# Five gate tiles instead of four held back for the end of attention, and a fourth raw weight buffer

## The chip, the cores and the metric

The kernel runs on one core of one Trainium2 chip. The metric is device time in microseconds for one launch, the median over several runs. The program names are those of the engines: TensorE (PE, with its weight loads as PEld), VectorE (DVE), ScalarE (ACT), GpSimd (POOL), and SyncE (SP), which issues nearly all DMAs from one queue (SPq).

## The reference

Two layers work on 528 tokens (16 learned ones and 512 of the sequence) of width 1024. Each layer normalises, makes one large input projection, mixes tokens in two ways, and adds the gated sum of both back:

```python
h = rmsnorm(h_res, norm_gain[l])
proj = h @ w_in[l]
u_pool, z_pool, c_q, c_kv, k_rope, z_mla, g_pool, g_mla = jnp.split(proj, IN_SPLIT_POINTS, axis=-1)
y_pool = (pool_mix(u_pool, pool_w_group[l], pool_scale[l]) * jax.nn.silu(z_pool)) @ pool_w_up[l]
o_mla = mla(c_q, c_kv, k_rope, pos, q_a_norm_gain[l], kv_a_norm_gain[l], w_q_b[l], w_kv_b[l],
            q_norm_gain[l], k_norm_gain[l])
y_mla = (o_mla * jax.nn.silu(z_mla)) @ mla_w_up[l]
merged = jax.nn.sigmoid(g_pool) * y_pool + jax.nn.sigmoid(g_mla) * y_mla
h_res = h_res + merged @ w_out[l]
```

`mla` is causal attention with 8 heads (96 query and key dimensions, 64 value dimensions). `pool_mix` takes means over windows of 2, 4, 8 and 16 tokens.

## The kernel before, in words

**Tiles.** Features lie on the 128 partitions, tokens along the free dimension. A projection to 128 output features is a "tile", named after its part of the layer: `u`, `zp`, `cq`, `pu`, `zm`, `gp0` to `gp7` (the pooling gate), `gm0` to `gm7` (the attention gate), `mu` (attention's up projection), `o` (the output). A gate tile has 8 blocks of 128 input features. Layer 0 takes the tokens in two halves of 264, each with a PSUM bank of its own; layer 1 drops the learned tokens and takes 512 at once.

**Every product is three matmuls.** Full precision comes from splitting weights and activations into a high and a low float32r part. `mm3` (lines 211 to 213) issues high x high, high x low and low x high. So a gate tile has 48 matmuls in layer 0 and 24 in layer 1.

**Weights.** `wload` brings 512 columns, half of a gate tile, from HBM into a `raw` buffer (three of them, line 140; the load is issued by SyncE on line 136), ScalarE makes the high part `whi` (line 206) and VectorE the low part `wlo` (line 207). There are three buffers each of `whi` and `wlo`. A raw buffer is free when line 207 has read it. Loads run four chunks ahead of the matmuls in the program. SyncE's queue is in order: a load that waits for its buffer holds back all that stands behind it.

**Filler.** `stream` is a generator of all projections in a fixed order; each `step` emits a few of its matmuls and moves a planner's clock `clk` by 1/2.4 ns per column. The attention code calls it in its gaps. `fill(ns, limit)` lets the clock run up by `ns` per call, but not past the end of the tile named `limit`; `fill_now(ns)` has no limit. `gap` (line 1159) calls `fill` with `FILL[layer]` and `RESERVE[layer]`. One head has four gaps, two in `head` and two in `go`, so a layer has 32. Whatever the gaps leave is run after the last head.

**One head.** `head` issues the scores of four query blocks in three PSUM banks `S`: blocks 1 and 3 (in part) in the first, block 2 in the second, the rest of block 3 and block 0 in the third. VectorE adds the mask and takes the row maximum (line 843), ScalarE takes the exponential (line 850), VectorE transposes in blocks of 32 (line 856). SyncE writes the result to HBM (`pdr`, line 916) and reads it back rearranged (`attE`, line 924), with the row sums by `rdr` (written on line 927, read on line 934). `parts` splits what came back (ScalarE line 972, VectorE line 973), and `pv` multiplies with the values (lines 994 and 997) into the one bank `o`. ScalarE and VectorE move its two halves together (lines 1002 and 1003). After each second head, one more matmul for the learned tokens follows (line 1009), which VectorE adds and gates (lines 1012 and 1013).

**The end of a layer's attention** (in `go`): the round trip of the last head through HBM is covered by `fill_now(TAIL[layer])`, then `parts`, 2600 ns more, and the last `pv`. What is left of `gm` follows, and then `mu`, which needs all heads.

**Banks.** The projections share four PSUM banks `mm`, used in turn. Those of `gp` are emptied by VectorE line 665, those of `gm` by VectorE line 1058.

**Order.** Within each engine the instructions run in the printed order. A scheduler with its own timeline sets it from the program's order and its dependencies, so a change of the gap lengths moves instructions on all engines.

The constants and `rawt` as they stand before are in the listing that follows.

Of the kernel before, what the change touches and what calls it, by code (L numbers as in the profile page):

```python
# [9 lines left out]
F32 = mybir.dt.float32  # L10
# [8 lines left out]
P = 128  # L19
# [31 lines left out]
G_H, G_CKV, G_CQ, G_QN, G_QR, G_KN, G_KR, G_PS = 0, 8, 10, 16, 17, 18, 19, 20  # L51
N_GAIN = 24

FILL = (2583.0, 2493.0)
RESERVE = ("gm3", "gm3")
LAG = 2000.0
TAIL = (9000.0, 9000.0)
SPL = 240
BACK = 7800.0
LATE = 13000.0  # L60
# [21 lines left out]
def trunk(ctx, tc, xT, xrow, mrow, pos, win, wkr, wqb, wkb, wvb, wgr, wpu, wmu, wout, gains, const, yT):  # L82
# [5 lines left out]
    wp = ctx.enter_context(tc.tile_pool(name="wp", bufs=2))  # L88
# [7 lines left out]
    def nm(s):  # L96
        uid[0] += 1
        return f"{s}_{uid[0]}"
# [38 lines left out]
        return raw  # L137

    def rawt():
        return wp.tile([P, 512], F32, tag="raw", name=nm("raw"), bufs=3)  # L140

    early.append(slot("rinv"))
    act.dma_start(early[0][:, 0:512], win[0, MT_CKV, :, 0:512])
    first = sp.dma_start(gn, gains)
    sp.dma_start(xb[:, 0, :T], xT[:, 0, :])
    early.append(fetch(win[0, MT_CKV + 1, :, 0:512], 512, rawt(), sp))
    sp.dma_start(xb[:, 1, :T], xT[:, 1, :])
    xt = [xb[:, k] for k in range(8)]
# [16 lines left out]
    def other_loads(made):  # L165
        for k in range(2, 8):
            behind(sp.dma_start(xb[:, k, :T], xT[:, k, :]), made)
            if k in (3, 4):
                raw = rawt()
                behind(sp.dma_start(raw, win[0, MT_CKV + k - 3, :, 512:1024]), made)  # L170
                early.append(raw)
        behind(sp.dma_start(cst, const), made)
        behind(sp.dma_start(posb[:, :T], pos.partition_broadcast(P)), made)
        dve.tensor_copy(maskw[:, 512 - P:], cst[:, C_MASK:C_MASK + P])
# [18 lines left out]
    def wload(src, n, spare, home=None):  # L193
        if home is not None:
            raw = home
            behind(sp.dma_start(raw, src), marks[-4])
        else:
            raw = early.pop(0) if early else fetch(src, n, rawt(), sp)
        loads[0] += 1
        marks.append(newest[0])  # L200
        if loads[0] <= 2 or spare:
            t = wide()
            hi, lo = t[:, 0:512], t[:, 512:1024]
        else:
            hi, lo = (wp.tile([P, 512], F32R, tag=t, name=nm(t), bufs=3) for t in ("whi", "wlo"))
        act.activation(hi[:, :n], raw[:, :n], AF.Copy)  # L206
        dve.tensor_sub(lo[:, :n], raw[:, :n], hi[:, :n].bitcast(F32))  # L207
        return hi, lo
# [87 lines left out]
    def fill(ns, limit):  # L296
        if due[0] is None:
            due[0] = clk[0]
        due[0] += ns
        while clk[0] < due[0] and limit not in done and step():  # L300
            pass

    def fill_now(ns):
        end = clk[0] + ns
        while clk[0] < end and step():
            pass
# [47 lines left out]
    class Layer:  # L354
# [804 lines left out]
        def gap(self):  # L1159
            fill(FILL[self.l], (self.l, RESERVE[self.l]))  # L1160

        def go(self, nxt):
# [54 lines left out]
            if not self.last:  # L1217
                self.meta_queries()
            fill_now(TAIL[self.l])
            late = self.parts(now)  # L1220
# [87 lines left out]
```

## Time and profile before

| | us |
|---|---|
| median of 3 runs | 753.75 |
| lowest and highest of them | 753.75, 754.27 |
| the profiled execution's own time | 755.48 |
| its span, first to last instruction | 753.7 |
| layer 0, TensorE, first score matmul of head 0 to the last of head 7's third bank | 175.63 to about 279.8 |
| layer 0, last P.V begins | 303.98 |
| layer 1, first masks to those of head 7 | 560.3 to 655.6 |

In the profile, busy times of matmuls overlap, since the next one starts while one drains; what a matmul costs is read from the distance of two starts. A row of the timeline gives start, duration, engine, line, operation and tile. "Idle before" in square brackets names what ended the idle time.

### The profile page before, as it was taken

To read this page: it belongs to the slowest core of one execution; us is meant where nothing else is said; L and a number is where in the kernel's file an instruction comes from. 1 tells how busy PE (TensorE), PEld (TensorE's weight loads), DVE (VectorE), ACT (ScalarE), POOL (GpSimd) and SP (SyncE) were. 2 spreads that over 40 slices of the span, in tenths; PEclk is the share of its full clock that TensorE was granted. 3 is DMA by queue.
4 is the path that set the end of the run, shared out by engine and by line. 5 is a ranking of instruction groups with operands and counts; after the bars stand their busy time and mean duration, and the time that the engine had idled before them with its cause. 6 is when DMAs were issued, how large, how long until landed. Compare 5 with 4: busy or idle time off the path is not lost.

```text
span 753.7 us, 14317 instructions
## 1 busy us (share of the span) xinstructions
PE 748.1 (99%) x5010; PEld 681.9 (90%) x5010; DVE 562.3 (75%) x1214; ACT 395.2 (52%) x864; POOL 241.8 (32%) x294
## 2 busy tenths in 40 slices
PE   9999999999999999999999999999999999999998
PEld 9999899999999999999997898887788888887887
DVE  5588777658999987694367478678589999966942
ACT  6755656554656555543254456455445665554321
POOL 2126404704552520161130264038043526102400
PEclk9999999999999999999999999999999999999999
DMA  8633223434766576425643332233356666763462
GB/s 280 179 103 118 70 81 91 112 96 142 206 163 177 170 202 176 129 91 165 183 135 91 108 113 73 82 91 107 105 151 216 181 175 189 203 167 98 129 223 87
DMA packets 72798, 106.55 MB, mean 141 GB/s; under 512 B 14051, under 2 KB 34915, under 8 KB 72726
## 3 DMA queue, kind: packets, MB, share of 16 engines
q1 hardware_dynamic: 72582, 105.38, 47.8%
q8 instruction: 39, 0.64, 0.4%
q14 instruction: 33, 0.27, 0.1%
q10 hardware_dynamic: 144, 0.26, 0.1%
HBM read 89.76 MB, written 15.85 MB: 140 GB/s over the span
## 4 chain that ended last, share of the span: by engine, by line
PE 94%; DMA 4%; SPq 1%; DVE 1%; ACT 0%; issue 0%; ACTq 0%; DVEq 0%
PE mm L211 28%; PE mm L213 28%; PE mm L212 28%; PE S L211 2%; PE S L213 2%; PE S L212 2%; DMA raw<-wmu 1%; PE o L994 1%; DMA rdr<-rs 1%; PE o L997 1%; PE S L891 1%; PE S L538 1%; PE S L504 0%; DMA raw<-win 0%; DMA cq<-rdr 0%; DMA xb<-xT 0%
## 5 line engine op out<-in xcount | busy, mean ns | idle before, releaser
L213 PE MATMUL mm<-hh,wlo 128*128 128x264 f32 (+2 forms) x1072 | 337.0, 316 | 0.0
L212 PE MATMUL mm<-hl,whi 128*128 128x264 f32 (+2 forms) x1072 | 336.4, 315 | 0.0
L211 PE MATMUL mm<-hh,whi 128*128 128x264 f32 (+2 forms) x1072 | 336.3, 315 | 0.0
L207 DVE TENSOR_TENSOR wlo<-raw,whi 128x512 fp32r<-128x512 f32 (+2 forms) x239 | 179.6, 754 | 87.5 <-ACT whi L206 83.9
L206 ACT ACTIVATE whi<-raw 128x512 fp32r<-128x512 f32 (+2 forms) x239 | 143.0, 600 | 167.3 <-PE mm L212 133.2
L211 PEld LDWEIGHTS mm<-hh,whi 128*128 128x128 f32 x1072 | 201.4, 188 | 14.1 <-DVE vt L704 0.8
L212 PEld LDWEIGHTS mm<-hl,whi 128*128 128x128 f32 x1072 | 201.6, 188 | 13.0
L213 PEld LDWEIGHTS mm<-hh,wlo 128*128 128x128 f32 x1072 | 200.9, 188 | 12.3
L652 POOL TENSOR_TENSOR racc<-racc,tmp 128x264 f32<-128x264 f32 (+1 forms) x15 | 14.9, 993 | 117.7 <-ACT tmp L651 117.7
L1069 POOL TENSOR_TENSOR tmp<-tmp,xb 128x264 f32<-128x264 f32 (+1 forms) x24 | 27.7, 1166 | 41.8 <-DVE tmp L1067 39.7
L821 POOL CAST qhl<-q 32x528 fp32r<-32x528 f32 (+1 forms) x32 | 27.6, 876 | 40.5 <-PE S L891 39.1
L843 DVE CUSTOM_DVE_ANT_0 S<-S,maskw,nqs 128x240 f32<-128x240 f32 (+4 forms) x80 | 37.9, 493 | 1.5 <-PE S L213 1.3
L211 PE MATMUL mm<-cq,whi 128*128 128x264 f32 (+1 forms) x108 | 34.7, 321 | 0.0
L212 PE MATMUL mm<-th,whi 128*128 128x264 f32 (+1 forms) x108 | 34.6, 321 | 0.0
L213 PE MATMUL mm<-u,wlo 128*128 128x264 f32 (+1 forms) x108 | 34.5, 320 | 0.0
L212 PE MATMUL mm<-cq,whi 128*128 128x264 f32 (+1 forms) x108 | 34.5, 321 | 0.0
L213 PE MATMUL mm<-cq,wlo 128*128 128x264 f32 (+1 forms) x108 | 34.5, 321 | 0.0
L211 PE MATMUL mm<-u,whi 128*128 128x264 f32 (+1 forms) x108 | 34.5, 319 | 0.0
L938 POOL TENSOR_TENSOR u<-u,cq 128x512 f32<-128x512 f32 x8 | 12.9, 1616 | 64.6 <-DMA cq<-rdr 41.2
L853 POOL COPY pm<-cq 128x16 f32<-128x16 f32 x32 | 17.9, 559 | 44.4 <-ACT cq L850 42.3
L850 ACT ACTIVATE cq<-S,bia 128x400 f32<-128x400 f32 (+2 forms) x48 | 24.4, 512 | 13.9 <-DVE bia L904 12.8
L973 DVE TENSOR_TENSOR attE<-attE,th 128x640 fp32r<-128x640 f32 x32 | 25.6, 828 | 6.1 <-ACT th L972 6.1
(305 smaller groups left out, 1401.2 us busy)
## 6 DMA issues: line engine op xcount, KB each, us to landing
raw<-win SPq DMA_DIRECT2D x143, 256.0 KB, 3.5
pdr<-attD SPq DMA_DIRECT2D x16, 640.0 KB, 3.6
attE<-pdr SPq DMA_DIRECT2D x64, 160.0 KB, 3.6
raw<-wout SPq DMA_DIRECT2D x32, 256.0 KB, 3.0
raw<-wpu SPq DMA_DIRECT2D x16, 256.0 KB, 2.7
raw<-wmu SPq DMA_DIRECT2D x16, 256.0 KB, 2.7
raw<-wqb SPq DMA_DIRECT2D x12, 256.0 KB, 2.6
xb<-xT SPq DMA_DIRECT2D x8, 264.0 KB, 5.6
```

What stands on the lines that cost most here:

```text
L206: act.activation(hi[:, :n], raw[:, :n], AF.Copy)
L207: dve.tensor_sub(lo[:, :n], raw[:, :n], hi[:, :n].bitcast(F32))
L211: first = pe.matmul(out, wh, xh, start=start, stop=False)
L212: pe.matmul(out, wh, xl, start=False, stop=False)
L213: newest[0] = pe.matmul(out, wl, xh, start=False, stop=stop)
L652: self.acc_last = gp.tensor_add(self.acc[:, a:b], self.acc[:, a:b], t[:, :b - a])
L821: gp.tensor_copy(d[r0:r0 + 32, x0:T], f[gq:gq + 32, x0:T])
L843: return dve.tensor_tensor_reduce(out=sv, in0=sv, in1=mask, scale=nqs[:, i, h:h + 1], scalar=3e38, op0=ALU.add, op1=ALU.min, accum_out=bia ...
L850: act.activation(pv, sv, AF.Exp, scale=-1.0, bias=bia[:, i:i + 1], accum_out=rs[:, c:c + 1])
L853: gp.tensor_copy(pm[:, i, 16 * odd:16 * odd + 16], pt[i][:, 0:NM])
L973: dve.tensor_sub(got[:, a:b], f[:, a:b], hi[:, a:b].bitcast(F32))
L1069: gp.tensor_add(t[:, :b - a], t[:, :b - a], self.am[m][:, a:b])
```

## The change

```diff
-FILL = (2583.0, 2493.0)
-RESERVE = ("gm3", "gm3")
+FILL = (2217.0, 2145.0)
+RESERVE = ("gm2", "gm2")
 LAG = 2000.0
-TAIL = (9000.0, 9000.0)
+TAIL = (14300.0, 14000.0)
...
     def rawt():
-        return wp.tile([P, 512], F32, tag="raw", name=nm("raw"), bufs=3)
+        return wp.tile([P, 512], F32, tag="raw", name=nm("raw"), bufs=4)
```

Each of the 32 gaps of a layer is shortened by 366 (layer 0) and 348 (layer 1) ns of the planner's clock. The gaps may run the stream to the end of `gm2` instead of `gm3`, so that `gm3` to `gm7` are kept for the end instead of `gm4` to `gm7`. The stretch before the last head's `parts` grows by 5300 and 5000 ns; a gate tile is 5280 ns in layer 0 and 5120 in layer 1 on that clock. And raw weight chunks get a fourth buffer. No operation is added to or taken from TensorE; the printed orders have 4871 rows for it in both.

What the orders show at three places. In a row stand line, operation, what is written <- what is read, and the shape. The first is TensorE in layer 0, head 1: the scores of its third bank (`S_2817` now) and the filler around them, the two token halves of a `zm` tile (`mm_2760`, `mm_2761`). Now:

```order
L213 MATMUL mm_2760<-hh_16_156,wlo_2757 128x264
L211 MATMUL S_2817<-kh_2474,qhl_109 128x288
L212 MATMUL S_2817<-kl_2475,qhl_109 128x288
L213 MATMUL S_2817<-kh_2474,qhl_110 128x288
L891 MATMUL S_2817<-kh_2474,qhl_109 128x144
L891 MATMUL S_2817<-kl_2475,qhl_109 128x144
L891 MATMUL S_2817<-kh_2474,qhl_110 128x144
L891 MATMUL S_2817<-kh_2474,qhl_109 16x16
L891 MATMUL S_2817<-kl_2475,qhl_109 16x16
L891 MATMUL S_2817<-kh_2474,qhl_110 16x16
L211 MATMUL mm_2760<-hh_18_158,whi_2756 128x264
```

Before, these scores stood 15 filler matmuls later, after the end of `mm_2761`. So it is in most heads of layer 0: scores come after less filler.

The second place is where head 6's scores begin in layer 0. On TensorE, now (`mm_3766` and `mm_3767` are the two token halves of one gate tile, `mm_3774` is the learned tokens' matmul of heads 2 and 3, the `S` rows are the first pass of head 6's scores):

```order
L213 MATMUL mm_3766<-hh_18_158,wlo_3763 128x264
L1009 MATMUL mm_3774<-racc_3551,vb_1257 128x512
L211 MATMUL S_3789<-kh_3616,qhl_107 128x272
L211 MATMUL S_3798<-kh_3616,qhl_107 128x400
L211 MATMUL S_3877<-kh_3616,qhl_107 128x288
L211 MATMUL mm_3767<-hh_4_144,whi_3721 128x264
```

With four banks in turn, `mm_3774` takes the bank of `mm_3526`, and `mm_3767` that of `mm_3640`. VectorE's rows that follow the emptying of `mm_3526`, now:

```order
L667 SCALAR_TENSOR_TENSOR xb<-tmp_3630,xb 128x264
L1012 TENSOR_TENSOR tmp_3483<-mm_3774,tmp_3483 128x512
L665 TENSOR_TENSOR tmp_3739<-mm_3640,rinv_585 128x264
L910 RECIPROCAL rs_3560<-rs_3560 128x4
L665 TENSOR_TENSOR tmp_3756<-mm_3641,rinv_585 128x264
L1013 TENSOR_TENSOR tmp_3483<-tmp_3483,u_461_2706 128x512
```

Before, the learned tokens' matmul of these heads (`mm_3884`) stood amid the filler of a tile half, the next tile half opened the bank of `mm_3698`, and VectorE emptied that among the masks of head 5:

```order
L665 TENSOR_TENSOR tmp_3760<-mm_3697,rinv_585 128x264
L843 ISA S_3772,bia_3657<-S_3772,maskw,nqs_2282 128x288
L843 ISA bia_3657 128x1
L665 TENSOR_TENSOR tmp_3825<-mm_3698,rinv_585 128x264
L1003 TENSOR_TENSOR tmp_3570<-o_3800,tmp_3570 64x512
```

What moved: the emptying of `mm_3640` now stands behind the row that reads `mm_3774`, and TensorE comes to `mm_3767` after less filler.

The third place is SyncE's queue at the end of attention in layer 1: row sums of the last head (`rdr`), the learned tokens (`racc`), the last chunk of `gm7` (`win`), the first chunks of `mu` (`wmu`). Before:

```order
L927 DMA rdr_143<-rs_8559 128x4
L136 DMA raw_8853<-win 128x512
L136 DMA raw_8872<-wmu 128x512
L934 DMA cq_1558_8707<-rdr_143 64x512
L136 DMA raw_8901<-wmu 128x512
L955 DMA racc_8817<-mdr 32x4x128 x3
```

Now:

```order
L927 DMA rdr_143<-rs_8474 128x4
L955 DMA racc_8732<-mdr 32x4x128 x2
L934 DMA cq_1540_8621<-rdr_143 64x512
L955 DMA racc_8732<-mdr 32x4x128
L136 DMA raw_8853<-win 128x512
L136 DMA raw_8880<-wmu 128x512
```

The last chunk of `gm7` and the first of `mu` moved from ahead of the read of `rdr`, which waits for its write to land, to behind it.

## The prediction

> **What bounds the kernel now.** I read the page first, then who waited for whom on TensorE, then busy time by stage, then single instructions at the places where TensorE came closest to a wait. The page:
>
> ```profile
> span 753.7 us, 14317 instructions
> PE 748.1 (99%) x5010; PEld 681.9 (90%) x5010; DVE 562.3 (75%) x1214; ACT 395.2 (52%) x864; POOL 241.8 (32%) x294
> ```
>
> TensorE is never free for long, and the matmuls are the same before and after the change. So only pauses between them can be won or lost. The waits of TensorE (waiter, what it waited for, us in total, times, longest), and the timeline of TensorE around the two that lie in the program (start, us, instruction, idle before it):
>
> ```profile
> PE mm L211 <- DVE cq L1058: 1.1, 1, 1.1
> PE S L994 <- ACT th L972: 0.2, 1, 0.2
> ...
> 303.50 0.28 PE L213 MATMUL mm<-hh,wlo 128*128 128x264 f32 x1
> 303.98 0.51 PE L994 MATMUL S<-th,vt 128*128 128x512 f32 x1 [0.19 <-ACT th L972]
> ...
> 686.16 0.40 PE L213 MATMUL mm<-q,th 128*128 128x512 f32 x1
> 687.70 0.47 PE L211 MATMUL mm<-q,whi 128*128 128x512 f32 x1 [1.14 <-DVE cq L1058]
> ```
>
> Starts tell the price of a matmul, since each overlaps the next. In a stretch without waits, 25 steps of 264 columns and 9 steps of 512 (first and last row of each):
>
> ```profile
> 297.03 0.28 PE L211 MATMUL mm<-hh,whi 128*128 128x264 f32 x1
> ...
> 300.07 0.28 PE L212 MATMUL mm<-hl,whi 128*128 128x264 f32 x1
> ...
> 661.71 0.39 PE L212 MATMUL mm<-hl,whi 128*128 128x512 f32 x1
> ...
> 663.79 0.39 PE L212 MATMUL mm<-hl,whi 128*128 128x512 f32 x1
> ```
>
> 3.04 / 25 = 0.1216 us and 2.08 / 9 = 0.231 us. The step 303.50 to 303.98 is 0.48 us, so 0.36 is lost there; 686.16 to 687.70 is 1.54, so 1.31 is lost. About 1.67 us is all that better cover at the two ends of attention can bring.
>
> The second engine matters because of its share inside attention. Busy time by stage, columns as in the header row:
>
> ```profile
> core 0: us, PE busy (x) PEld busy (x) DVE busy (x) ACT busy (x) POOL busy (x), PEclk, DMA share, GB/s
> 175.63:258.36 82.73, 82.73 (x673) 82.07 (x672) 77.46 (x203) 48.96 (x122) 36.41 (x53) 1.00 0.58 166
> 180.60:257.58 76.98, 76.98 (x627) 76.36 (x626) 74.24 (x197) 46.70 (x118) 36.31 (x52) 1.00 0.60 170
> 180.60:291.06 110.46, 110.46 (x895) 109.32 (x894) 105.52 (x289) 68.20 (x176) 42.68 (x65) 1.00 0.62 176
> 175.63:291.48 115.85, 115.85 (x939) 114.71 (x938) 108.44 (x293) 70.31 (x180) 42.79 (x66) 1.00 0.61 174
> 560.30:655.60 95.30, 95.30 (x475) 80.38 (x474) 92.96 (x224) 60.37 (x145) 41.06 (x62) 1.00 0.64 186
> ```
>
> VectorE is busy 105.52 of 110.46 us in the heads of layer 0 and 92.96 of 95.30 in those of layer 1. TensorE has no pause there only because VectorE is just fast enough. How just, two places of layer 0 show, where a matmul opens a PSUM bank that VectorE has emptied a moment before (VectorE row and TensorE row of each):
>
> ```profile
> 257.16 0.42 DVE L665 TENSOR_TENSOR tmp<-mm,rinv 128x264 f32<-128x264 f32 x1
> 258.39 0.28 PE L211 MATMUL mm<-hh,whi 128*128 128x264 f32 x1
> ...
> 290.65 0.41 DVE L1058 TENSOR_TENSOR cq<-mm,rinv 128x264 f32<-128x264 f32 x1
> 291.48 0.28 PE L211 MATMUL mm<-hh,whi 128*128 128x264 f32 x1
> ```
>
> The bank is empty at 257.58 and used at 258.39 (0.81 us to spare); at 291.06 and 291.48 (0.42). That the row pairs share a bank is inferred from the rotation of four banks in the order of first use.
>
> **The change part by part.**
>
> *Less filler between the heads.* FILL falls by 366 and 348 per gap, and each layer has 32 gaps. The printed orders tell what that moves. In layer 0, from head 0's first score block to the second place above, TensorE has 733 filler matmuls before and 685 now: 48 fewer, one gate tile, 48 x 0.1216 = 5.8 us. To the first place (in the changed order the second token half of a gate tile, opened as head 6's scores begin) it is 529 before and 457 now, 72 fewer or 8.8 us, against which three hoisted score matmuls of 272, 400 and 288 columns cost about 0.4 us. So TensorE reaches these places 8.3 and 5.7 us sooner.
>
> VectorE must have done nearly as much by then. Its groups between the heads of layer 0, and two of layer 1 (busy us, mean ns):
>
> ```profile
> L207 DVE TENSOR_TENSOR wlo<-raw,whi 128x512 fp32r<-128x512 f32 x29 | 20.9, 722 | 0.1
> L843 DVE CUSTOM_DVE_ANT_0 S<-S,maskw,nqs 128x272 f32<-128x272 f32 (+4 forms) x40 | 19.3, 491 | 0.6 <-PE S L213 0.5
> L667 DVE SCALAR_TENSOR_TENSOR xb<-tmp,xb 128x264 f32<-128x264 f32 x16 | 7.4, 465 | 0.6 <-ACT tmp L666 0.6
> L665 DVE TENSOR_TENSOR tmp<-mm,rinv 128x264 f32<-128x264 f32 x16 | 6.7, 423 | 0.1
> L1003 DVE TENSOR_TENSOR tmp<-o,tmp 64x512 f32<-64x512 f32 x7 | 4.8, 684 | 0.1
> L1058 DVE TENSOR_TENSOR cq<-mm,rinv 128x264 f32<-128x264 f32 x8 | 3.4, 419 | 0.1
> ...
> L207 DVE TENSOR_TENSOR wlo<-raw,whi 128x512 fp32r<-128x512 f32 x26 | 18.3, 704 | 0.7 <-ACT whi L206 0.7
> L973 DVE TENSOR_TENSOR attE<-attE,th 128x640 fp32r<-128x640 f32 x12 | 9.6, 834 | 0.0
> ```
>
> At the second place VectorE has 287 instructions ahead before and 285 now: three L207 (2.2 us) and two L1058 (0.8) fewer, one each of L1003, L310 and L1013 more (about 0.7 each): 0.9 less. At the first, two L207, three L665 and two L667 fewer (1.4 + 1.3 + 0.9 = 3.6), and an L1003, an L1012, two masks (L843), two transposes and small ones more, about 3.1: 0.5 less. So the spare time becomes 0.81 - 8.3 + 0.5 = -7.0 us at the first place and 0.42 - 5.7 + 0.9 = -4.4 at the second. These are not added: a pause at the first lets VectorE catch up for the second, so the larger decides. The late bank is emptied behind one more wait: VectorE's L1012 stands ahead of that L665, and needs the L1009 matmul of TensorE; behind it queue the other gate evacuations and the next weight split.
>
> What softens it is VectorE's idle time, 76.98 - 74.24 = 2.7 us up to the first place; if a late VectorE never waits, 7.0 shrinks to 4.3. Bounds for layer 0: 4.3 and 7.0. I take 5.5, between them, since part of that idle time is the wait for ScalarE's exponentials, which come no sooner.
>
> In layer 1, up to head 7's last scores the order has 13 filler matmuls fewer (13 x 0.231 = 3.0 us) and one L1009 more (0.2), and VectorE loses one L207 and two L973 (0.7 + 1.7 = 2.4). The two move almost together: 0, from -0.4 to +1.
>
> *TAIL and RESERVE.* The tile that leaves the heads is run before the last head's P.V. In layer 0 it covers the 0.36 us: -0.36. In layer 1 the loss of 1.31 us is another chain, on the chain of waits (start, us) and in SyncE's queue:
>
> ```profile
> 669.51 4.02 DMA rdr<-rs
> 673.61 0.45 SPq L934
> 674.15 5.58 DMA raw<-wmu
> 679.75 0.64 ACT th L206
> 680.41 0.79 DVE th L207
> 681.22 2.70 DMA raw<-wmu
> ...
> 686.86 0.70 DVE cq L1058
> ...
> 671.30 0.43 SPq L136 DMA_DIRECT2D raw<-win  x1
> ...
> 678.03 0.69 DVE L207 TENSOR_TENSOR wlo<-raw,whi 128x512 fp32r<-128x512 f32 x1 [2.33 <-ACT whi L206]
> ...
> 679.68 0.40 PE L213 MATMUL mm<-hh,wlo 128*128 128x512 f32 x1
> ```
>
> SyncE waits for the small write rdr, and the wmu chunk behind it lands at 679.73. Its split frees a raw buffer, only then is the next chunk asked for (681.22), and VectorE's gate evacuation L1058 stands behind that chunk's split. *The fourth raw buffer* takes away the link at 681.22: a gain of 1.31 at most. But the order also moves the last win chunk and the first wmu chunk behind the wait for rdr. By then VectorE is about 2.4 us ahead of before, so rdr would return near 671.2 instead of 673.6, and the win chunk goes out near 672.2 instead of 671.30; its split has 679.68 - 678.72 = 0.96 us to spare, which that uses up. I take -0.7, from -1.3 to +1. At the start and elsewhere the buffer only lets loads go sooner, where TensorE does not wait: 0.
>
> *Sum.* 5.5 + 0 - 0.36 - 0.7 = +4.4 us. Against the profiled execution (span 753.7, its own time 755.48) that is 758.1 of span; its time lies 1.73 above the median of the runs shown, so I put the difference on the median: 753.75 + 4.4 = **758.2 us**. The likeliest case's own range is 4.3 - 1.7 = +2.6 to 7.0 + 1 + 1 = +9 at the outermost, mostly 756 to 761.
>
> **The rivals.** *A, absorbed:* the row pairs do not share the bank I think, and the weight splits, which are made chunks ahead, lend VectorE the time; then only the gains stay, 753.75 - 1.67 = 752.1. It decides if VectorE takes back all its idle time of 110.46 - 105.52 = 4.9 us, which turns -4.4 at the second place into +0.5. For it: the stretch ends in a part with little VectorE work. Against it: the first place stays late even then. Chance 0.12.
>
> *B, a draw:* the pause is there but small, 1 to 3 us, and the two gains pay for it: 753.75 + 2 - 1.67 = 754.1. Chance 0.08.
>
> *C, late in both layers:* in layer 1, too, the spare times between the heads are used up (VectorE is 97.5% busy there), and the win chunk behind rdr comes late: 7.0 + 1 + 1 - 0.36 = +8.6, 762.4. Chance 0.06.
>
> *D, a slow array after the pause:* if a pause of some 5 us in one piece made TensorE come back at half pace for as long, it would lose another 2.5 us: 760.7. All stages above show a granted clock of 1.00, but none of them has such a pause. Chance 0.05. [...]
>
> *E, the same sign without the fourth buffer's gain:* the split weights have three buffers still, so the chunk comes no sooner, and the 1.31 stays: 753.75 + 5.5 - 0.36 = 758.9. It is counted in the forecast's chance of 0.69.
>
> **How the numbers follow.** About 0.2% (1.5 us) is what a measurement of this kernel can tell from no change: faster means below 752.2, slower above 755.3. A gives faster, B the same, the forecast and C and D slower; a little of each neighbour goes over the edge: faster 0.12, same 0.09, slower 0.79. The range should leave out most of A (0.12) and the top of C: 753.0 to 761.0.
>
> **What would show it.** Right: TensorE has waits inside layer 0's heads, from about head 3 on and above all where head 6's scores begin, released by VectorE (L665, L207, L1058), 4 to 7 us in all; VectorE is 97% busy or more from the first to the last head; the 0.36 us at the last P.V. of layer 0 is gone; and at the mu matmuls of layer 1 the wait for L1058 is shorter. Wrong: no TensorE wait above 0.5 us in layer 0's heads (A), waits of the same size in layer 1's heads (C), a clock below 1.00 (D), or pauses released by DMA rather than VectorE, since then the running sums of VectorE are not what decides.

## The result, and the profile after

The changed kernel is slower: 764.45 us median of four runs (764.12 to 764.82), against 754.01 for the kernel before beside it (753.75 to 755.52), a ratio of 1.0132 with a 95% interval of 1.012 to 1.0143. The forecast was 758.2 with a range up to 761.0: right in sign, too small by 6 us. The profiled execution took 764.82 us. Its page:

```profile
span 763.0 us, 14322 instructions
PE 752.2 (99%) x5010; PEld 684.6 (90%) x5010; DVE 560.9 (74%) x1214; ACT 396.6 (52%) x864; POOL 239.9 (31%) x294
```

TensorE has the same 5010 instructions and is busy 4.1 us longer (752.2 against 748.1): matmuls themselves took longer somewhere, for which the forecast's sum had no term. The waits of TensorE in it (waiter, what it waited for, us in total, times, longest):

```profile
PE mm L211 <- DVE tmp L1012: 2.0, 1, 2.0
PE mm L1009 <- DVE tmp L665: 1.6, 1, 1.6
PE mm L211 <- DVE tmp L665: 1.1, 1, 1.1
...
PE mm L1042 <- ACT whi L206: 0.8, 1, 0.8
PE S L994 <- ACT th L972: 0.5, 1, 0.5
PE mm L213 <- DVE wlo L207: 0.4, 1, 0.4
```

The first three lie in layer 0's heads. TensorE there, and where the pace comes back (start, us, instruction, idle before it):

```profile
222.54 0.28 PE L213 MATMUL mm<-hh,wlo 128*128 128x264 f32 x1
223.90 0.36 PE L211 MATMUL mm<-hh,whi 128*128 128x264 f32 x1 [1.08 <-DVE tmp L665]
...
251.13 0.28 PE L213 MATMUL mm<-hh,wlo 128*128 128x264 f32 x1
253.05 0.50 PE L1009 MATMUL mm<-racc,vb 96*128 96x512 f32 x1 [1.63 <-DVE tmp L665]
253.39 0.60 PE L211 MATMUL S<-kh,qhl 96*128 96x272 f32 x3
255.99 0.59 PE L211 MATMUL mm<-hh,whi 128*128 128x264 f32 x1 [2.00 <-DVE tmp L1012]
...
261.44 0.30 PE L211 MATMUL mm<-hh,whi 128*128 128x264 f32 x1
```

By the distance of starts, less the 0.12 us of a step (0.44 for the three score matmuls of 272, 400 and 288 columns), 1.24, 1.79 and 2.16 us are lost at the three places, 5.19 in all. A fourth pause, 0.93, follows at line 1042 at 293.5. VectorE at the second and third place:

```profile
251.83 0.69 DVE L1003 TENSOR_TENSOR tmp<-o,tmp 64x512 f32<-64x512 f32 x1
252.56 0.43 DVE L665 TENSOR_TENSOR tmp<-mm,rinv 128x264 f32<-128x264 f32 x1
252.91 0.70 DVE L310 TENSOR_TENSOR kl<-tmp,kh 128x528 fp32r<-128x528 f32 x1
253.52 0.70 DVE L856 STREAM_TRANSPOSE attD<-cq 128x512 f32<-128x512 f32 x1
...
254.53 0.81 DVE L667 SCALAR_TENSOR_TENSOR xb<-tmp,xb 128x264 f32<-128x264 f32 x1
255.26 0.68 DVE L1012 TENSOR_TENSOR tmp<-mm,tmp 128x512 f32<-128x512 f32 x1
255.86 0.42 DVE L665 TENSOR_TENSOR tmp<-mm,rinv 128x264 f32<-128x264 f32 x1
```

Line 665 empties a bank at 252.99, and line 1009 starts at 253.05. Its own bank is emptied by line 1012, which stands behind a split, a transpose and a gate row and ends at 255.94; the next tile half starts at 255.99, before the L665 below has ended. So it did not wait for that L665, and what fits its start is the bank of the learned tokens' matmul.

The matmuls that took longer lie where the granted clock is low. Busy time by stretch (columns as in the header):

```profile
core 0: us, PE busy (x) PEld busy (x) DVE busy (x) ACT busy (x) POOL busy (x), PEclk, DMA share, GB/s
250.00:254.60 4.60, 2.36 (x16) 1.81 (x14) 4.54 (x13) 2.47 (x8) 3.18 (x6) 1.00 0.39 124
254.60:261.40 6.80, 5.41 (x24) 5.41 (x25) 5.39 (x13) 2.61 (x6) 1.22 (x2) 0.50 0.67 208
261.40:270.00 8.60, 8.60 (x73) 8.55 (x72) 6.68 (x16) 4.73 (x10) 2.53 (x3) 1.00 0.46 138
```

For 6.8 us the granted clock is 0.50. From 255.99 to 261.44 TensorE makes 24 steps in 5.45 us instead of 24 x 0.1216 = 2.92: 2.5 us lost. At the two ends of attention:

```profile
305.23 0.28 PE L212 MATMUL mm<-hl,whi 128*128 128x264 f32 x1
305.36 0.40 PE L994 MATMUL S<-th,vt 128*128 128x512 f32 x1
...
679.06 0.39 PE L212 MATMUL mm<-hl,whi 128*128 128x512 f32 x1
679.96 0.50 PE L994 MATMUL S<-th,vt 128*128 128x512 f32 x1 [0.50 <-ACT th L972]
...
692.45 0.40 PE L212 MATMUL mm<-kn,whi 128*128 128x512 f32 x1
693.28 0.50 PE L213 MATMUL mm<-q,wlo 128*128 128x512 f32 x1 [0.43 <-DVE wlo L207]
```

Layer 0's last P.V starts without loss (-0.36, as forecast). In layer 1 the old pause of 1.31 is gone, but 0.66 and 0.60 stand in its place. These account for 8.2 of the 9.3 us by which the two profiled spans differ: pauses of layer 0 5.19 + 0.93, clock 2.5, last P.V -0.36, layer 1 -0.05. Of the other 1.1, half was there before the first head (head 0's scores at 176.2 against 175.63); the rest was not found in any one place, and no cause is claimed for either. The medians differ by 10.4 us, 1.1 more than the spans, because the profiled execution of the kernel before lay 1.5 us above its median and that of the change 0.4.

### The profile page after: what moved, and what is told of

The parts are those of the page before. It is cut to its first block, busy times and chain, and to the rows that moved or that the text cites. A ratio compares the mean times of both kernels' runs of the same rounds, so it can differ in the third digit from the quotient of the medians.

```text
span 763.0 us, 14322 instructions
## 1 busy us (share of the span) xinstructions
PE 752.2 (99%) x5010; PEld 684.6 (90%) x5010; DVE 560.9 (74%) x1214; ACT 396.6 (52%) x864; POOL 239.9 (31%) x294
## 4 chain that ended last, share of the span: by engine, by line
PE 89%; DVE 4%; DMA 4%; issue 1%; ACT 1%; SPq 0%; POOL 0%; ACTq 0%; DVEq 0%; POOLq 0%
PE mm L213 27%; PE mm L211 27%; PE mm L212 27%; PE S L212 2%; PE S L213 2%; PE S L211 2%; DMA raw<-wmu 1%; DMA attE<-pdr 1%; DMA raw<-win 1%; PE o L997 1%; PE o L994 1%; DVE wlo L207 1%; PE S L538 1%; DVE attD L856 1%; PE S L891 1%
## 5 line engine op out<-in xcount | busy, mean ns | idle before, releaser
L821 POOL CAST qhl<-q 32x528 fp32r<-32x528 f32 (+1 forms) x32 | 24.7, 787 | 39.5 <-PE S L891 38.3
L938 POOL TENSOR_TENSOR u<-u,cq 128x512 f32<-128x512 f32 x8 | 15.1, 1885 | 66.6 <-DMA cq<-rdr 30.9
L973 DVE TENSOR_TENSOR attE<-attE,th 128x640 fp32r<-128x640 f32 x32 | 28.6, 917 | 6.9 <-ACT th L972 6.9
L850 ACT ACTIVATE cq<-S,bia 128x400 f32<-128x400 f32 (+2 forms) x48 | 24.4, 512 | 10.1 <-DVE bia L904 8.7
```

The source lines that it names most:

```text
L821: gp.tensor_copy(d[r0:r0 + 32, x0:T], f[gq:gq + 32, x0:T])
L850: act.activation(pv, sv, AF.Exp, scale=-1.0, bias=bia[:, i:i + 1], accum_out=rs[:, c:c + 1])
L938: behind(gp.tensor_mul(z, z, rb[:, 0:512].rearrange("p (q i) -> p i q", i=4)), newest[0])
L973: dve.tensor_sub(got[:, a:b], f[:, a:b], hi[:, a:b].bitcast(F32))
```

## The experiments

Each was timed beside the kernel before, whose medians were 753.70 to 754.06. "Pauses" are what TensorE lost in waits of 0.5 us or more in the profiled execution, in layer 0's heads and their end unless another place is named; "half clock" is the length of the stretch at 0.50 in the same execution. Other executions of the same kernel can differ in it: the four runs of e18_later_own_bank took 756.55 us at a mean granted clock of 1.000, 759.17 and 760.44 at 0.998 and 760.94 at 0.996; of e6_qlpool three runs at 1.000 still took 762.61 to 763.19.

| run | us | ratio, 95% interval | pauses, us | half clock, us |
|---|---|---|---|---|
| e1_raw4 | 753.62 | 0.9999, 0.9989 to 1.0008 | none | none |
| e4_layer1 | 754.48 | 1.0006, 0.9997 to 1.0015 | none | none |
| e8_gaps_kept | 754.78 | 1.0013, 1.0004 to 1.0023 | none (0.33) | none |
| e3_layer0 | 761.25 | 1.01, 1.0083 to 1.0117 | 0.69, 1.56, 2.16, 0.72 | 3.4 |
| e2_hold | 761.58 | 1.0103, 1.0088 to 1.0118 | 0.69, 1.01, 2.17, 0.66; layer 1: 0.72 | 3.4 |
| e5_again | 763.02 | 1.0117, 1.0102 to 1.0133 | 1.24, 1.70, 2.16, 0.56; layer 1: 0.71 | 6.8 |
| e6_qlpool | 763.11 | 1.0125, 1.0108 to 1.0141 | 1.43, 1.28, 1.31, 1.08; layer 1: 2.00 | 3.4 twice |
| e7_one_tile | 766.56 | 1.0164, 1.0147 to 1.0181 | 3.09, 0.76, 0.73, 0.66, 1.96; layer 1: 1.25, 0.86 | 3.4 twice |
| e9_own_bank | 759.62 | 1.0069, 1.0048 to 1.009 | 0.69, 1.28, 0.76; layer 1: 0.55 | 3.4 |
| e10_own_bank_ql | 759.92 | 1.0082, 1.0054 to 1.011 | 1.43, 1.32, 1.13, 0.58; layer 1: 0.63 | none |
| e11_own_bank_mid | 759.46 | 1.007, 1.0051 to 1.0088 | 2.01, 0.68; layer 1: 2.20 | none |
| e12_dose | 763.87 | 1.0126, 1.0104 to 1.0149 | 0.59, 1.42, 4.18; layer 1: 1.19, 0.52 | 6.8 |
| e13_no_low_split | 756.12 | 1.0032, 1.002 to 1.0044 | 1.70 | none |
| e14_extra_vector | 755.46 | 1.0022, 1.0012 to 1.0031 | none (1.12 at 57 us) | none |
| e15_small_dose | 758.45 | 1.0076, 1.0054 to 1.0097 | 1.00, 2.20 | none |
| e16_dose_later | 755.75 | 1.0025, 1.0016 to 1.0035 | 0.78 | none |
| e17_later | 759.20 | 1.0063, 1.0046 to 1.008 | 0.72, 2.28; layer 1: 0.50 | 3.4 |
| e18_later_own_bank | 759.80 | 1.007, 1.0046 to 1.0094 | 0.64, 1.28, 0.76; layer 1: 1.53 | 6.8 |

### Which part of the change costs

`e1_raw4`, the kernel before with the fourth raw buffer alone:

```diff
-        return wp.tile([P, 512], F32, tag="raw", name=nm("raw"), bufs=3)
+        return wp.tile([P, 512], F32, tag="raw", name=nm("raw"), bufs=4)
```

> The kernel before, with the fourth raw buffer alone. Theory 1 (the shorter gaps in layer 0 do all the harm: VectorE falls behind, TensorE pauses for about 5 us, and the halved clock after the pauses costs about 3 more): no harm from the buffer, and at best the 1.31 us at the mu matmuls of layer 1 is won: 752.5 to 754.5, no clock of 0.50. Theory 2 (the buffer's earlier loads disturb SyncE's queue and the start, and cost part of the 10 us): 755 or more, with the first matmul of layer 0 late by about 0.5 us as in the changed kernel (4.94 against 5.14 started, but 6.23 against 6.07 for the third tile row).

`e2_hold`, the change without that buffer:

```diff
-        return wp.tile([P, 512], F32, tag="raw", name=nm("raw"), bufs=4)
+        return wp.tile([P, 512], F32, tag="raw", name=nm("raw"), bufs=3)
```

> The change without the fourth raw buffer (three as before). VectorE's and TensorE's orders in layer 0's heads are as in the changed kernel, so theory 1 gives the same pauses (5.2 us in layer 0's heads) and the same low clock: 763 to 766. Theory 2 gives less than 762.

`e3_layer0`, the change with layer 1's numbers as before:

```diff
-FILL = (2217.0, 2145.0)
-RESERVE = ("gm2", "gm2")
+FILL = (2217.0, 2493.0)
+RESERVE = ("gm2", "gm3")
-TAIL = (14300.0, 14000.0)
+TAIL = (14300.0, 9000.0)
```

> The change with layer 1's three numbers as before, layer 0's as changed, four raw buffers. Theory 1: 763 to 765, the pauses and the low clock all there. If layer 1's part cost something too (theory 3): 761 to 763.

`e4_layer1`, the mirror image: FILL (2583, 2145), RESERVE ("gm3", "gm2"), TAIL (9000, 14000).

> The change with layer 0's three numbers as before, layer 1's as changed, four raw buffers. Theory 1: 752.5 to 754.5, no pause between the heads of either layer, clock 1.000. Theory 3: 755 to 757.

`e5_again` is the change once more, with a comment line added and nothing else.

> The changed kernel once more, nothing altered, for its second profile: does the low clock last 6.8 us each time, or one or two stretches of 3.4 us as the pauses fall? If it is chance: a time between 761.5 and 765 and a low clock of 3.4 or 6.8 us. If it belongs to the kernel: 764 to 765 and 6.8 us again. The pauses in layer 0's heads 4.5 to 5.5 us in both cases.

`e8_gaps_kept`, the change with the gaps as long as before:

```diff
-FILL = (2217.0, 2145.0)
+FILL = (2583.0, 2493.0)
```

> The changed kernel with the gaps as before (FILL 2583 and 2493), RESERVE, TAIL and the fourth buffer as changed. Theory 1: pauses of at most 1.3 us near head 7's end, no low clock, 753 to 755.5. If holding five tiles back costs by itself: 757 or more.

The buffer alone and layer 1 alone cost nothing that can be measured; layer 0 alone costs 7.2 us; and with the gaps as before, the same RESERVE, TAIL and buffer cost 1.0. So without the shorter gaps in layer 0 most of the loss is not there. (No run shortens them with RESERVE and TAIL as before.) In `e8_gaps_kept` the fifth tile is held back too, but out of the gaps behind the last scores, where the limit stops the stream: from head 0's first score matmul to head 7's last, its trace has 661 filler matmuls, as that of before, and the trace of the change 559.

Two of these expectations missed. `e2_hold` and `e3_layer0` came out below the 763 us that theory 1 asked for, in the bands of the theories that blame the buffer and layer 1; yet the buffer alone and layer 1 alone, `e1_raw4` and `e4_layer1`, came out by theory 1. `e2_hold` and `e3_layer0` lie 1.4 to 3.2 us below the change and its repetition, which themselves differ by 1.4 us. Their profiles show 0.69 instead of 1.24 us at the first pause and one stretch of 3.4 us at half clock instead of 6.8. What decides about the second stretch in a given run is not shown; the one run of `e3_layer0` at a mean clock of 0.995 took 762.36 us, the three at 0.998 took 760.49 to 761.53.

### VectorE's load, or the order

`e6_qlpool` gives one subtraction for each head's queries to GpSimd:

```diff
-            dve.tensor_sub(ql[n0:n0 + 64, x0:T], src, qh[n0:n0 + 64, x0:T].bitcast(F32))
+            gp.tensor_sub(ql[n0:n0 + 64, x0:T], src, qh[n0:n0 + 64, x0:T].bitcast(F32))
```

> The changed kernel with the low part of the queries (L814, 0.9 us per head on VectorE) made by GpSimd instead. Theory 1 (VectorE's throughput is what TensorE waits for): the running sums say that 4 to 5 us come off VectorE's load up to the first place, so no pause above 0.5 us is left in layer 0's heads, the clock stays 1.000, and the time is 752.5 to 755.5. If the pauses come from the order of the instructions or a DMA rather than from VectorE's load: the pauses stay, 760 or more.

`e7_one_tile` makes half of the cut:

```diff
-FILL = (2217.0, 2145.0)
+FILL = (2418.0, 2333.0)
```

> The changed kernel with gaps shortened by one gate tile's worth only (FILL 2418 and 2333; 165 and 160 less per gap than before). Running sums: pauses of 1.5 us between heads 3 and 4 and 2.4 us between heads 5 and 6, 3.9 in all. Without a low clock 756 to 758; with one after the second pause 757.5 to 760.

By theory 1 both missed. The first took nothing back and, by its own words, spoke for the order of the instructions or a DMA rather than VectorE's load. From 240 to 254.5 us VectorE is busy 13.45 of its 14.5 us, where the change has 14.37, and line 665 still releases pauses of 1.28 and 1.31 us there. The longest waits of its TensorE in attention, the first of them in layer 1:

```profile
PE mm L1009 <- DMA racc<-mdr: 1.8, 1, 1.8
PE S L211 <- ACT cq L850: 1.3, 1, 1.3
PE mm L1009 <- DVE tmp L665: 1.1, 1, 1.1
```

The second is slower than the whole change. Its longest pause, in TensorE's timeline, is again the matmul behind line 1009:

```profile
227.84 0.51 PE L1009 MATMUL mm<-racc,vb 96*128 96x512 f32 x1
231.16 0.36 PE L211 MATMUL mm<-hh,whi 128*128 128x264 f32 x1 [2.81 <-DVE tmp L1012]
```

From this came a second theory (T4 in the expectations; T1 is the first, that VectorE as a whole is late): line 1009 takes one of the four filler banks, and its emptying stands in VectorE's queue behind a backlog.

### Another bank for the learned tokens' matmul

The edit moves line 1009 out of the four filler banks into the bank `o`, which it then shares with P.V: `e9_own_bank` on the change; `e10_own_bank_ql` and `e11_own_bank_mid` the same on the two kernels above:

```diff
-                    m = mmt()
+                    m = pp.tile([P, 512], F32, tag="o", name=nm("o"), bufs=1)
```

> The kernel after, with the learned tokens' matmul (line 1009) put into the bank o of the P.V products instead of one of the four banks mm. Theory T4 (the pauses come because line 1009 takes a filler bank and its emptying on VectorE, line 1012, stands behind a backlog): the waits 'mm L211 <- DVE tmp L1012' and 'mm L1009 <- DVE tmp L665' vanish, nothing over 1 us takes their place in layer 0's heads, the clock stays at 1.00, 754 to 757 us. Theory T1 (VectorE as a whole is late between the heads after the cut of FILL, the bank is only where it shows): the same 4 to 6 us turn up at other waits for VectorE (wlo, o, mm behind line 665), 759 to 765 us.

> Own bank for line 1009 and line 814's subtraction on GpSimd together. If both theories hold in part (VectorE late AND the filler bank behind line 1012), only both together take the pauses away: 753 to 756 us, clock 1.00. By T4 alone no better than with the own bank only; by T1 alone, no better than 763.1, the time of the subtraction's move by itself.

> The kernel with FILL at 2418 and 2333 (half of the cut) and own bank for line 1009. With the bank shared it took 766.6 us, with pauses of 3.1 and 2.0 us at matmuls that waited for line 1012. T4: both go, 754 to 757 us. T1: the sums of this order leave some 2 us of pauses elsewhere and, in one piece, a stretch of half clock: 756 to 759 us; over 760 us speaks against both.

Neither theory comes out whole. The edit is worth 3 to 7 us in all three (764.45 or 763.02 to 759.62, 763.11 to 759.92, 766.56 to 759.46), and yet some 6 us over the kernel before stay, in T1's band for `e9_own_bank`. But taking work from VectorE on top (`e10_own_bank_ql`) gives nothing more, which its expectation reads as T4 alone, and `e11_own_bank_mid` lies just above T1's band, far from T4's. The edit also makes the scheduler set a new order, so its gain is not shown to be the bank's alone. TensorE's timeline of `e9_own_bank` shows where the rest is lost:

```profile
249.30 0.39 PE L213 MATMUL mm<-hh,wlo 128*128 128x264 f32 x1 [0.52 <-DVE wlo L207]
250.63 0.29 PE L211 MATMUL S<-kh,qhl 96*128 96x272 f32 x1
252.03 0.51 PE L1009 MATMUL o<-racc,vb 96*128 96x512 f32 x1 [1.12 <-DVE tmp L1003]
253.03 0.39 PE L211 MATMUL mm<-hh,whi 128*128 128x264 f32 x1 [0.49 <-DVE tmp L665]
```

Within 4 us TensorE waits for a weight split, for the bank of P.V and for the emptying of a gate's bank, all of them VectorE's, which is busy 14.35 of the 14.50 us from 240 to 254.5: the backlog is there whichever bank line 1009 takes.

### Small doses

`e12_dose` has FILL at (2500, 2145), `e15_small_dose` at (2560, 2145), else as the change. `e16_dose_later` is `e12_dose` with the learned tokens' matmuls further behind (T4' in the expectations is the theory that these matmuls, of lines 1009 and 1042, are issued too short a time after the VectorE work that feeds them):

```diff
-                after((3 if p == 3 else 2) * LAG, part2)
+                after(4 * LAG, part2)
...
-            after(2 * LAG, rest)
+            after(4 * LAG, rest)
```

> The kernel after with FILL of layer 0 at 2500 instead of 2217 (83 of the 366 ns cut), layer 1 as after. T1 (a deficit that grows with the cut): the pauses of layer 0's heads shrink to 0 to 1.5 us, no half clock, 754 to 756.5 us. T4 (where line 1009 and 1012 fall in the order decides, not the amount): the time does not follow the dose, 757 us or more.

> The kernel after with FILL of layer 0 at 2560 (23 of the 366 ns cut, 0.7 us of filler less over the layer), layer 1 as after. T1: pauses of at most 0.7 us more than with FILL unchanged (754.8): 754.5 to 756 us. If any change of the order costs what 2500 cost (763.9): 758 us or more.

> The kernel with FILL of layer 0 at 2500, which took 763.9 us with a pause of 4.2 us at line 1042, and the matmuls of lines 1009 and 1042 put 8000 ns of the planner's clock behind their VectorE work instead of 4000 (6000 for the last pair). T4': the pauses at these lines go, 754 to 757 us. T1: a deficit of 2.7 us at most (83 ns x 32) stays, at other matmuls: 757 us or more.

The time does not follow the dose: cuts of 23, 83, 165 (`e7_one_tile`) and 366 ns per gap in layer 0 give 758.45, 763.87, 766.56 and 764.45 or 763.02 us. The three runs of this section all miss the bands of T1, a deficit that grows with the cut, and `e16_dose_later` meets that of T4'. (Part of the 758.45 is the clock: three of the four runs of `e15_small_dose` show a mean below 1.000, and the fourth, the profiled one, took 757.65.) The longest pause of `e12_dose` is at line 1042. Its VectorE, with the last rows ahead of that matmul, and its TensorE:

```profile
293.76 0.67 DVE L310 TENSOR_TENSOR kn<-tmp,q 128x512 fp32r<-128x512 f32 x1
...
295.13 0.64 DVE L207 TENSOR_TENSOR wlo<-raw,whi 128x512 fp32r<-128x512 f32 x1
295.70 0.67 DVE L1003 TENSOR_TENSOR tmp<-o,tmp 64x512 f32<-64x512 f32 x1
296.40 0.21 DVE L1036 TENSOR_TENSOR mh<-smt,mh 32x64 fp32r<-32x64 f32 x1
```

```profile
292.46 0.34 PE L213 MATMUL mm<-hh,wlo 128*128 128x264 f32 x1
296.76 0.99 PE L1042 MATMUL mm<-mh,vb 96*128 96x16 f32 x4 [3.96 <-DVE mh L1036]
```

Line 1042 is due 4000 ns of the planner's clock behind the last small VectorE row that feeds it (line 1036), whatever VectorE's queue holds by then; here a weight split, the P.V sum and others stood ahead. In `e15_small_dose`, too, the longest pause, 2.20, is at line 1042, which starts at 293.66, with line 1036 at 293.30. With 8000 ns the pause is gone and 8.1 of the 10.1 us come back: in `e16_dose_later` line 1036 runs at 292.55 and line 1042 at 294.80.

### More and less work for VectorE

`e13_no_low_split`, on the change:

```diff
+        if one:
+            return hi, hi
         dve.tensor_sub(lo[:, :n], raw[:, :n], hi[:, :n].bitcast(F32))
...
-                return wload(g_.src[:, c:c + n], n, g_.spare)
+                return wload(g_.src[:, c:c + n], n, g_.spare, one=g_.name[0] == 0 and g_.name[1][:2] in ("zm", "gp", "gm"))
```

> The kernel after, but in layer 0 the weights of zm, gp and gm have no low part: line 207 is left out for them and line 213 multiplies with the high part instead (the same matmuls, some 19 us of VectorE work less in the heads of layer 0; the output is less exact). T1 (VectorE is late between the heads): no pause over 0.5 us from 175 to 295 us, no half clock, 752.5 to 755.5 us (layer 1's end still loses up to 1.3). T4' (matmuls that are issued a fixed time after their VectorE work, lines 1009 and 1042, and the order that the scheduler makes): pauses stay at these two lines, 757 us or more.

It leaves out the low part of those weights, so its output is less exact; it serves as a measurement only. With 40 VectorE instructions fewer (530.2 us busy against 560.9), 8 of the 10 us are gone. (The edit does more than lighten VectorE: no matmul waits for these low parts any more, raw buffers come free without line 207, and the order is a new one. It does not tell load from order.) What stays is one pause of 1.70, again at the matmul behind the learned tokens' (1012 and 668 are lines 1009 and 665 in this listing). Its time of 756.12 lies between the bands of T1 and T4'. Its busy time, and its TensorE:

```profile
180.50:291.00 110.50, 108.94 (x878) 107.33 (x877) 90.08 (x271) 69.74 (x181) 35.78 (x65) 1.00 0.63 181
240.00:254.50 14.50, 12.96 (x102) 12.50 (x102) 14.32 (x38) 9.24 (x25) 6.82 (x12) 1.00 0.67 207
```

```profile
249.23 0.40 PE L1012 MATMUL mm<-racc,vb 96*128 96x512 f32 x1
251.17 0.39 PE L214 MATMUL mm<-hh,whi 128*128 128x264 f32 x1 [1.54 <-DVE tmp L668]
```

VectorE is busy only 90.08 of 110.50 us in the heads, but still 14.32 of 14.50 from 240 to 254.5, where the work of heads 4 and 5 meets.

`e14_extra_vector`, on the kernel before:

```diff
             turn(1)
             turn(2)
+            if self.l == 0 and h < 6:
+                dve.tensor_sub(vscr, tcos[:, 0:512], tsin[:, 0:512])
```

> The kernel before, with one more VectorE instruction of 128x512 (some 0.67 us, written to a buffer that nobody reads) in each of heads 0 to 5 of layer 0: 4.0 us of VectorE work, nothing else. T1: the spare time of 0.4 to 0.8 us in the heads is used up, pauses of 1 to 3.6 us behind VectorE and perhaps one stretch of half clock (+1.7): 755 to 759 us. T4' (only the shorter gaps put the matmuls too close): 753.5 to 754.5 us.

This run says nothing on the question. The rows of the added tile (count, durations in ns, first and last start) show that the scheduler, free to do so, put all six far ahead of the heads:

```profile
L883 DVE TENSOR_TENSOR vscr<-tcos,tsin x6: 681/690/1134, 52.2 to 57.7; 128x512 f32<-128x512 f32 x6
```

### The whole change, with the learned tokens' matmuls later

`e17_later` is the change with the edit of `e16_dose_later`, `e18_later_own_bank` has line 1009 in the bank `o` too.

> The kernel after with lines 1009 and 1042 put 8000 ns of the planner's clock behind their VectorE work instead of 4000 (6000 for the last pair), as in the run that took the dose of 2500 from 763.9 to 755.8. T4' (these matmuls stand too close behind VectorE once the gaps are shorter): the pauses at lines 1009, 1012 and 1042 go, 754 to 758 us. T1 (a deficit of VectorE in layer 0's heads that the order only moves; by the sum of the durations in this order up to 7.7 us at a bank behind line 665, near 230 us): 758 to 764 us.

> As the run before, and line 1009's matmul in the bank o as well. T4': neither a late line 1009 nor a filler bank held by it is left, 754 to 757 us, no half clock. T1: by the sums of this order some 4 us of pauses stay at the low parts and at the bank o, 757 to 762 us.

By their bands both speak for T1. The first gives back about half (759.20), and the bank on top gives nothing more (759.80). In `e17_later` line 1009 comes at 257.23, after the crowded stretch, and the pause remains, on TensorE's timeline:

```profile
250.94 0.29 PE L211 MATMUL S<-kh,qhl 96*128 96x272 f32 x1
253.34 0.39 PE L211 MATMUL mm<-hh,whi 128*128 128x264 f32 x1 [2.11 <-DVE tmp L665]
```

No version was measurably faster than the kernel before.

## Why the prediction was right in sign and wrong in size

*What bounds the kernel:* right. Every pause of over a microsecond in layer 0's heads after the change was released by VectorE, at about head 3 and where head 6's scores begin, as the forecast had it; leaving out weight splits takes 8 of 10 us away (`e13_no_low_split`), and without the cut of FILL the pauses do not come (`e8_gaps_kept`). The sign "97% busy or more from the first to the last head" did not come: VectorE is busy 103.36 of 110.46 us there, 94%, and by the prediction's own row it was 95.5% before. A share of the whole is too coarse. From 240 to 254.5 us VectorE is full before the change as after it:

```profile
240.00:254.50 14.50, 14.50 (x119) 14.27 (x118) 14.25 (x37) 8.76 (x22) 8.05 (x10) 1.00 0.56 161
240.00:254.50 14.50, 12.36 (x96) 11.66 (x94) 14.37 (x37) 8.96 (x23) 9.52 (x14) 1.00 0.60 178
```

The third pair of numbers is VectorE's, 14.25 us before and 14.37 after. In `e13_no_low_split` it is full there even with a seventh of its work in the heads gone. The masks of heads 4 and 5, whose work meets there, come 7 to 8 us apart, while 20 to 24 us lie ahead of head 4.

*Less filler, 5.5 us from bounds of 4.3 and 7.0:* 5.19 up to 256 us, 6.1 with line 1042. Size and places were right, the bank was not: the tile half behind head 6's scores did not wait for the emptying of `mm_3640` but, by the times above, for line 1012. And the agreement is partly luck: the same sums of VectorE's durations, made for other orders, were off by 5 us both ways (0 to 1.5 expected of `e12_dose`, 6.2 found; up to 7.7 of `e17_later`, 3.0 found). Such sums hold neither the times at which VectorE's inputs come nor the 4000 ns that the planner allows between line 1036 and line 1042.

*The step that failed is the sum, where it gave a pause only its own length.* Rival D, at 0.05, had the missing term: after pauses TensorE ran 6.8 us at half clock, 2.5 us here and 2.5 in the rival. D's half pace after a pause was the author's supposition, which no trace of before shows; what the change showed is a granted clock of 0.50 from 254.64 to 261.46 us. "None of them has such a pause" was true of the stages before, and therefore no argument that the clock would stay. D belonged in the likeliest case, since that case itself forecast a pause of some 5 us. That D's 2.5 us agree is chance: D makes the low clock last as long as one pause of 5 us, and the trace shows 6.8 us at half clock that begin inside the pause of 2.16, right behind one of 1.79. With D's term the forecast would have been 760.7, inside the range but still short. Of the 6.2 us by which 764.45 exceeds 758.2, the clock is 2.5, larger pauses 0.6, the missing gain in layer 1 0.65, and 1.1 have no known cause. The last 1.4 come from setting a difference of spans upon a median: the profiled execution before lay 1.73 us above that median, the one after only 0.37 above its own.

*The gains:* the 0.36 at layer 0's last P.V came. Of the 0.7 hoped for in layer 1, 0.05 came. The fourth buffer alone does take away the pause of 1.31 (it is absent in `e1_raw4`), but the new order does so without the buffer (it is absent in `e2_hold`), and waits for `th` (line 972) and for a low part (line 207) take 1.26 in its place. The outcome is rival E's, by another way. Nor does the buffer's gain show in the median of `e1_raw4`.

*Layer 1, 0 from -0.4 to +1:* right; no pause between its heads, and nothing measurable for the layer alone. Rivals A and B fell with the pauses, C with layer 1.

Shown by the runs: the loss needs the shorter gaps in layer 0; the pauses end when VectorE gets to a row that stood behind others in its queue, where the work of heads 4 and 5 meets (and of 6 and 7); and the granted clock halved at some of them (0.50 for 3.4 or 6.8 us at a time, in the change and nine of the runs). Argued, not shown alone: the filler bank that line 1009 holds, 3 to 5 us of the change with its share of half clock, since the edit also changes the order and gives nothing once lines 1009 and 1042 stand later. Open: why some 5 us resist both edits at these lines, whether VectorE's load or its order decides (`e6_qlpool` and `e10_own_bank_ql` speak against the load, `e13_no_low_split` for it but not cleanly), and which property of the scheduler's order it is. A cut of 23 ns (with layer 1's, which alone costs nothing measurable) already takes 3.7 us more than none, so it is not the amount of filler alone.

## What to carry to other kernels

Where a second engine is full in stretches, read the stretch, not the stage: a mean share hides where two pieces of its work meet, and shortening the cover, the filler that hides its waits, can move the first engine straight into it. A matmul whose operand or bank comes from that engine should be placed by how long its queue is, not at a fixed distance; and if something has to be held back, take it from where nothing waits (`e8_gaps_kept`: 1 us) instead of from every gap (10 us). Give forecast pauses their price in clock as well: here 5.19 us of pauses came with 6.8 us at a granted clock of 0.50, which cost 2.5 us more.

## What the runs showed of the hardware

In attention, the granted clock of these traces fell to 0.50 at pauses of TensorE and was back at 1.00 after 3.4 or 6.8 us. In that of the change it is 0.50 from 254.64 to 261.46 us, from inside the pause of 2.16. In `e3_layer0` it followed pauses of 1.56 and 2.16 us; the busy times around them:

```profile
250.20:256.00 5.80, 2.40 (x16) 1.86 (x16) 5.74 (x13) 2.49 (x9) 4.33 (x7) 1.00 0.60 226
256.00:259.46 3.46, 3.46 (x19) 3.46 (x18) 2.80 (x8) 1.85 (x6) 0.00 (x0) 0.51 0.55 136
```

A single pause of 1.70 us was not followed by it in `e13_no_low_split` (mean granted clock 1.000 in the profiled execution), nor one of 1.42 in `e12_dose`. Around 2.0 to 2.2 us in one piece it went either way: half clock in `e6_qlpool` layer 1 after 2.00; none in the profile of `e15_small_dose` after 2.20 (mean 1.000). Pauses of 0.69, 1.28 and 0.76 within 4.5 us brought it (`e9_own_bank`, 3.4 us at 0.50). What decides between these cases was not shown.
